# Half-tile weight buffers three tiles ahead, and seven products instead of eight in one more column group

## The chip, the cores and the metric

The kernel runs on one core of a Trainium2 chip. The time is device microseconds of one launch; the kernel before took 945.35 us (median of 3 runs, 945.0 to 945.57). A profile is one execution recorded by the hardware, on which every engine's instructions have a start and a duration.

## The reference, cut to what matters

The program is a two-layer encoder on 256 tokens of width 1024, all in float32. A layer has a gated feed-forward block, attention, and a second feed-forward block:

```python
x = x + 0.5 * swiglu(rms_norm(x, ffn1_norm[l]), ffn1_w_gate[l], ffn1_w_up[l], ffn1_w_down[l])
h = rms_norm(x, mix_norm[l]);  proj = h @ w_in[l]          # then two kinds of attention, and @ w_out[l]
x = x + 0.5 * swiglu(rms_norm(x, ffn2_norm[l]), ffn2_w_gate[l], ffn2_w_up[l], ffn2_w_down[l])

def swiglu(h, w_gate, w_up, w_down):
    return (jax.nn.silu(h @ w_gate) * (h @ w_up)) @ w_down
```

The hidden width is 2816. So there are four feed-forward blocks, and their weights (three matrices of 1024 x 2816 each) are by far most of what is read and multiplied.

## The kernel before, in words

**Precision.** Every operand of a matrix product is split in two, a rounded high part and the remainder (low). A product is three matmuls: high x high, low x high, high x low. ScalarE makes the high part of a weight (a cast, `act.copy`), VectorE the low part (a subtraction), in `emit_split` (line 167). The two are in buffers named `whi` and `wlo`, three of each, each of a whole tile.

**Weight tiles.** A tile is 512 rows of a weight matrix by 512 columns, 1 MB, laid out as 128 partitions x 4 x 512. One list, `specs`, holds the tiles in the order in which TensorE uses them. `emit_dma` loads a tile into one of six `raw` buffers; `ahead` (line 198) issues loads, preparations and splits; `weights` (line 219) is called when a tile's use begins and has the splits issued up to `LOOK = 2` tiles further. Each split is issued as two instructions of 128 x 1024 on ScalarE and two on VectorE.

**A feed-forward block** (`ffn`, line 547) goes over the hidden columns in five groups of 512 (numbers 0 to 4) and a last one of 256. In group n the gate and up products are made (4 tiles x 4 row blocks x 2 token blocks x 3 = 96 matmuls of 512 columns), and the hidden activations of group n-1 are transposed (`turn`) and multiplied by two tiles of the down matrix (`down`, 48 matmuls).

**Groups by seven products.** In groups 2 and 4 (`SEVEN`) gate and up are computed together as a 2 x 2 block product (token halves by input halves, input halves by gate and up) with seven block products in place of eight: 84 matmuls in place of 96 (`by_seven`, line 579). For this, seven weight tiles are split instead of four: four as loaded or with a second matrix added while it is loaded (`gather`, a load issued by GpSimd that adds into the buffer), three more made from buffers already there by additions on VectorE (`plus`, two instructions of 128 x 1024). The token operands that the sums need are made once for each block, in four steps during group 1 (`make_sums`, line 304). The order of the tiles in such a group, with the letters of `seven` (line 115): a, b, b again after an addition, the first down tile, d, d again after an addition, a again after a load has been added, c, the second down tile. The down product's first use needs the transposed activations of the group before, whose low part VectorE writes in `turn`.

**Order.** Outside the attention each engine runs its instructions in the order in which the program issues them (`keep_in_program_order`, line 50, which is why most instructions of the profile carry the line L50). So when `weights()` is called before a product, the splits that it triggers stand ahead, in ScalarE's and VectorE's queues, of everything that is issued after that product. In the attention a scheduler may reorder.

**Constants** for the attention are made in the first block, from `aside` at the start of group 3: eleven small instructions on VectorE, one exponential on ScalarE, and a transpose on TensorE (`attention_constants`, line 454).

Here are the functions that the change touches:

Of the kernel before, what the change touches and what calls it, by code (L numbers as in the profile page):

```python
# [14 lines left out]
P = 128  # L15
# [9 lines left out]
QA, KA, VA, QB, KB, VB = 0, 512, 640, 768, 1280, 1792  # L25
BIG = 1e33

LOOK, AHEAD = 2, 8
N_RAW, N_HI, N_LO = 6, 3, 3
N_S4 = 16  # L30
SEVEN = (2, 4)


@with_exitstack
def trunk(ctx: ExitStack, tc: tile.TileContext, x, n1, g1, u1, d1, nm, w_in, sink,
# [31 lines left out]
    def nm_(s):  # L67
        uid[0] += 1
        return f"{s}_{uid[0]}"
# [94 lines left out]
        if s.behind is not None:  # L164
            s.behind()

    def emit_split(i):
        s = specs[i]
        kn, n, raw = s.kn, s.n, raws[s.src]
# [3 lines left out]
        cuts = [0, kn // 2, kn] if i > 1 and (i not in fine or kn < 4) else [kn * j // 4 for j in range(5)]  # L173
        for a, b in zip(cuts, cuts[1:]):
            if n == D:
                views = [(t[0][:, a:b, c:c + 512], t[1][:, a:b, c:c + 512], t[2][:, a:b, c:c + 512])
                         for t in [(raw, hi, lo)] for c in (0, 512)]
            elif i not in paired:
                views = [(raw[:, a:b], hi[:, a:b], lo[:, a:b])]
            else:  # L180
                views = [(raw.rearrange("p k (s c d) -> p c k s d", s=2, c=2)[:, c, a:b],
                          hi.rearrange("p k (c s d) -> p c k s d", s=2, c=2)[:, c, a:b],
                          lo.rearrange("p k (c s d) -> p c k s d", s=2, c=2)[:, c, a:b]) for c in range(2)]
            for r_, h_, l_ in views:
                act.copy(h_, r_)
                dve.tensor_tensor(l_, r_, f(h_), op=ALU.subtract)
            if i < 2:
                yield
        for k in s.free:
            raws.pop(k)  # L190

    def emit_early(i):
        yield from emit_dma(i)
        yield from emit_split(i)

    at = dict(use=0, dma=2, prep=2, split=2)

    def ahead(n):

        n = min(n, len(specs) - 1)  # L200
        while True:
            if at["split"] <= n and at["prep"] > at["split"]:
                for _ in emit_split(at["split"]):
                    pass
                at["split"] += 1
            elif at["prep"] <= min(n + 1, len(specs) - 1) and at["dma"] > at["prep"] and \
                    (specs[at["prep"]].prep is None or at["split"] >= at["prep"]):
# [65 lines left out]
    class Norm:  # L273
# [115 lines left out]
    def take_x(k):  # L389
# [8 lines left out]
        elif k == 1:  # L398
            for e in (g, u, g, u):
                next(e)  # L400
            norm.pair(2)
            ahead(2)
            norm.pair(3)
        elif k == 2:
            ahead(3)
# [65 lines left out]
            dve.tensor_scalar_mul(gsub[:, l:l + 1], gcol[:, 48 + l:49 + l], 1.0 - lam_init[l])  # L471


    def tokens(accs, xs, w, k0, ks=range(4), first=0, last=KC - 1, order=None):

        hi, lo = w
        for k, t in (order or [(k, t) for k in ks for t in range(2)]):
            kk = k0 + k
            xv = xs[kk // 2][:, kk % 2]
            xh, xl = xv[:, t * P:(t + 1) * P], xv[:, S + t * P:S + (t + 1) * P]  # L480
            pe.matmul(accs[t], lhsT=xh, rhs=hi[:, k], start=kk == first, stop=False)
            pe.matmul(accs[t], lhsT=xl, rhs=hi[:, k], start=False, stop=False)
            pe.matmul(accs[t], lhsT=xh, rhs=lo[:, k], start=False, stop=kk == (last if isinstance(last, int) else last[t]))

    def split(dst, src, scale=None):

# [7 lines left out]

    def narrow(acc, w, j, xs, kcs, first, last):

        hi, lo = w
        for i, (wk, xk) in enumerate(kcs):
            wh = hi[:, wk, j * P:(j + 1) * P]
            wl = lo[:, wk, j * P:(j + 1) * P]  # L500
# [46 lines left out]
    def ffn(norm, aside=None, before=None, final=False):  # L547
# [19 lines left out]
            return h  # L567

        def prod(xo, w):
            hi, lo = w  # L570
            acc = bank()
            for k in range(4):
                xh, xl = xo(k)
                pe.matmul(acc, lhsT=xh, rhs=hi[:, k], start=k == 0, stop=False)
                pe.matmul(acc, lhsT=xl, rhs=hi[:, k], start=False, stop=False)
                pe.matmul(acc, lhsT=xh, rhs=lo[:, k], start=False, stop=k == 3)
            return acc

        def by_seven(h, g):
# [57 lines left out]
        if before is None:  # L637
            before = norm.late
        before(0)
        ws = (weights(), weights(LOOK - 1))  # L640
        for k in (0, 2):
            if k:
                before(1)
# [40 lines left out]
    def ffn_end(parts, last):  # L684
# [4 lines left out]
        w = {0: weights()}  # L689

        def group(h, order, a=None, c=slice(None), first=0):
            tokens(a or accs[h], hT, [t[:, :, c] for t in w[h]], G4, first=first, last=last[h], order=order)

        def tail(h, order=BY_TOKENS, a=None, c=slice(None)):
            tokens(a or accs[h], [None] * (2 * NGRP) + hE, [t[:, h, :, c] for t in w["rest"]], 4 * NGRP, last=last[h], order=order)
# [4 lines left out]
        w["rest"] = [t.rearrange("p k (h n) -> p h k n", h=2) for t in weights()]  # L700
        w[1] = weights(LOOK - 1)
        return group, tail

    def ffn_close(parts, nxt):
# [4 lines left out]
        for t in range(2):  # L709
            res.add(0, t)  # L710
        tail(1)
        ahead(at["use"] + LOOK - 1)
        group(1, [(1, t) for t in range(2)])
        for j in range(2):
            nxt.pair(j)
# [7 lines left out]
    def mix(l, norm, nxt_norm):  # L723
# [68 lines left out]
            return e  # L792


        s0, s1 = first_groups(norm, (weights(), weights(LOOK - 1)))
# [39 lines left out]
        vB = tp.tile([P, 2, 512], F32, tag="v", bufs=1, name=nm_("v"))  # L835
        vsl = [bank() for _ in range(2)]
        for k0 in (0, 4):
            hi, lo = weights()
            for k in range(4):
                kk = k0 + k  # L840
                xv = norm.xs[kk // 2][:, kk % 2]
                for t in range(2):
                    xh, xl = xv[:, t * P:(t + 1) * P], xv[:, S + t * P:S + (t + 1) * P]
                    pe.matmul(vsl[t], lhsT=xh, rhs=hi[:, k], start=kk == 0, stop=False)
                    pe.matmul(vsl[t], lhsT=xl, rhs=hi[:, k], start=False, stop=False)
                    pe.matmul(vsl[t], lhsT=xh, rhs=lo[:, k], start=False, stop=kk == KC - 1)
# [73 lines left out]
        res = Residual(nxt_norm, accs)  # L920

        def out_part(w, k0, h, order=None):
            tokens(accs[h], oT, [t.rearrange("p k (h n) -> p h k n", h=2)[:, h] for t in w], k0, range(2), 4, 3, order)

        w = weights()
        for h in range(2):
# [112 lines left out]
```

## Time and profile before

| | |
|---|---|
| Median of 3 runs | 945.35 us |
| Profiled execution | 945.94 us, of which the span of the trace is 944.2 us |
| TensorE (matmul) busy | 931.5 us, 99% |
| VectorE busy | 718.6 us, 76% |
| ScalarE busy | 538.1 us, 57% |
| DMA read | 184.32 MB at 196 GB/s over the span |
| Granted TensorE clock | 0.999 |

Busy shares are means over the whole span; a stage can look different. In the trace's timelines the first number is the start in us from the span's start, the second the duration of the row, then engine, line, operation, the names of what is written and read, and how many instructions the row merges. Matmuls overlap: one of 512 columns shows some 0.39 us, and the next starts 0.227 us after it. The four feed-forward blocks begin near 5, 290, 485 and 755 us.

### The profile page before, as it was taken

The numbers are of one execution on the slowest core, as the hardware profiler recorded it, in microseconds if no ns is written. First come the engines' busy times: TensorE is split into PE (matmuls) and PEld (weight loads), VectorE is DVE, ScalarE is ACT, GpSimd is POOL, SyncE is SP. The second block draws the span as 40 slices with busy tenths as digits, with TensorE's granted clock in tenths as the row PEclk, the third lists the DMA queues.
The fourth block names the chain that finished last, engine by engine and source line by source line (L and its number), as shares of the span: only waits on it lengthen the run. The fifth ranks groups of instructions, "written<-read, shape, count | busy, mean of one in ns | idle before, by whom it ended". The sixth has DMA issues, their size and how long they took to land.

```text
span 944.2 us, 12633 instructions
## 1 busy us (share of the span) xinstructions
PE 931.5 (99%) x4844; PEld 790.4 (84%) x4844; DVE 718.6 (76%) x1086; ACT 538.1 (57%) x853; POOL 40.6 (4%) x65
## 2 busy tenths in 40 slices
PE   8999999999999999999999999999999999999997
PEld 6887888899888887888888888888999888888886
DVE  5689779579856589679557995887796667995983
ACT  6647546567735547446554564656676464564653
POOL 0400000000000000000000000000000000000001
PEclk9999999999999999999999999999999999999999
DMA  9959868655424829958557498586551447497631
GB/s 336 338 140 286 246 178 303 190 179 136 134 90 144 256 92 286 293 133 306 185 179 223 97 329 243 148 300 186 170 168 56 139 174 223 104 346 241 151 118 45
DMA packets 106669, 186.19 MB, mean 197 GB/s; under 512 B 3438, under 2 KB 31152, under 8 KB 106608
## 3 DMA queue, kind: packets, MB, share of 16 engines
q1 hardware_dynamic: 96816, 167.27, 52.0%
q0 software_dynamic: 8704, 17.07, 10.5%
q10 hardware_dynamic: 1088, 1.05, 0.3%
q8 instruction: 38, 0.62, 0.3%
q14 instruction: 23, 0.19, 0.1%
HBM read 184.32 MB, written 1.05 MB: 196 GB/s over the span
## 4 chain that ended last, share of the span: by engine, by line
PE 82%; DVE 11%; ACT 4%; issue 2%; DMA 0%; ACTq 0%; POOLq 0%; POOL 0%; DVEq 0%
PE ps L50 82%; DVE wlo L50 6%; DVE tmp L50 3%; ACT whi L50 3%; DVE s L50 1%; ACT s L50 1%; DVE raw L50 0%; DMA xk<-in_x_dram 0%; ACT tmp L50 0%; DVE xk L50 0%; ACTq L50 0%; POOLq L1034 0%; POOL rf L50 0%; DVE rf L50 0%; DVEq L50 0%
## 5 line engine op out<-in xcount | busy, mean ns | idle before, releaser
L50 PE MATMUL ps<-whi,s 128*128 128x512 f32 (+1 forms) x2252 | 699.4, 391 | 2.0 <-DVE s L50 2.0
L50 DVE TENSOR_TENSOR wlo<-raw,whi 128x1024 fp32r<-128x1024 f32 (+2 forms) x440 | 433.8, 1034 | 97.7 <-ACT whi L50 95.1
L50 PEld LDWEIGHTS ps<-whi,s 128*128 128x128 f32 x2252 | 419.7, 188 | 88.4 <-DVE s L50 3.7
L50 ACT CAST whi<-raw 128x1024 fp32r<-128x1024 f32 (+2 forms) x440 | 372.0, 902 | 177.2 <-PE ps L50 117.7
L50 PE MATMUL ps<-wlo,s 128*128 128x512 f32 (+1 forms) x1126 | 438.1, 389 | 0.0
L50 PEld LDWEIGHTS ps<-wlo,s 128*128 128x128 f32 x1126 | 211.8, 188 | 43.9 <-DVE wlo L50 0.2
L50 PE MATMUL ps<-s,whi 128*128 128x256 f32 x448 | 82.7, 286 | 0.0
L50 PEld LDWEIGHTS ps<-s,whi 128*128 128x128 f32 x448 | 70.1, 192 | 1.1
L50 ACT CAST s<-ps 128x512 fp32r<-128x512 f32 x48 | 26.0, 589 | 66.0 <-PE ps L50 66.0
L50 PE MATMUL ps<-s,wlo 128*128 128x256 f32 x224 | 63.3, 283 | 0.0
L50 DVE TENSOR_TENSOR s<-ps,s 128x512 fp32r<-128x512 f32 x48 | 31.0, 685 | 41.5 <-ACT s L50 41.5
L50 PEld LDWEIGHTS ps<-s,wlo 128*128 128x128 f32 x224 | 42.9, 192 | 0.0
L50 ACT CAST s<-tmp 128x512 fp32r<-128x512 f32 (+1 forms) x22 | 13.2, 602 | 49.1 <-DVE tmp L50 49.1
L50 PE MATMUL ps<-ident,s 128*128 128x128 f32 x304 | 39.6, 273 | 0.0
L50 PEld LDWEIGHTS ps<-ident,s 128*128 128x128 f32 x304 | 35.1, 141 | 4.7
L50 POOL DMA_DIRECT2D raw<-in_ffn_w_up_dram x16 | 20.8, 1298 | 412.9 <-ACT whi L50 120.0
L50 DVE TENSOR_TENSOR raw<-raw,raw 128x1024 f32<-128x1024 f32 x32 | 37.6, 1218 | 0.0
L50 ACT ACTIVATE s<-s,negm 128x256 f32<-128x256 f32 x64 | 31.8, 501 | 7.4 <-DVE negm L50 7.4
L50 ACT ACTIVATE tmp<-ps,r 128x512 f32<-128x512 f32 (+1 forms) x32 | 19.9, 636 | 28.0 <-PE ps L50 27.9
L50 DVE SCALAR_TENSOR_TENSOR s<-ps,hr,tmp 128x512 f32<-128x512 f32 (+1 forms) x32 | 20.8, 681 | 13.4 <-PE ps L50 6.9
L50 ACT ACTIVATE s<-ps,gcol 128x256 fp32r<-128x256 f32 x48 | 19.3, 474 | 19.7 <-PE ps L50 19.7
L50 DVE SCALAR_TENSOR_TENSOR s<-ps,gcol,s 128x256 fp32r<-128x256 f32 x48 | 20.3, 477 | 13.1 <-ACT s L50 13.0
(104 smaller groups left out, 411.2 us busy)
## 6 DMA issues: line engine op xcount, KB each, us to landing
raw<-in_ffn_w_down_dram SPq DMA_DIRECT2D x44, 1024.0 KB, 5.2
raw<-in_ffn_w_gate_dram SPq DMA_DIRECT2D x39, 1024.0 KB, 6.2
raw<-in_ffn_w_up_dram SPq DMA_DIRECT2D x39, 1024.0 KB, 5.1
raw<-in_ffn_w_up_dram POOLq DMA_DIRECT2D x16, 1024.0 KB, 9.1
raw<-in_w_in_dram SPq DMA_DIRECT2D x14, 1024.0 KB, 5.1
raw<-in_ffn_w_gate_dram SPq DMA_DIRECT2D x8, 512.0 KB, 3.8
raw<-in_ffn_w_up_dram SPq DMA_DIRECT2D x8, 512.0 KB, 5.0
raw<-in_w_in_dram SPq DMA_DIRECT2D x8, 512.0 KB, 4.5
```

Of the source, the lines that this page charges most:

```text
L50: ins = issue(*a, **k)
```

## The change

Four things change together.

1. The split weights live in 14 buffers of half a tile (seven pairs of high and low) instead of six of a whole tile. `emit_split(i, j)` splits one half; `ahead` counts in halves. When a tile's use begins the halves up to six further are issued (`HALVES`), and when its second half is first used (`part`) one more. This is up to three tiles ahead, where it was two.
2. `SEVEN` becomes (2, 3, 4): group 3 of each block goes by seven products too.
3. The four sums of x are kept in buffers that the attention uses for other things (tags `q` and `v`), and the common pool `s4` has 14 buffers instead of 16.
4. `AHEAD`, how many tiles further the load list is looked at, becomes 10 instead of 8; the `raw` buffers stay six.

Some splits change form: the four tiles with the last 256 rows of the down matrices are split in 2 instructions of 1024 elements instead of 4 of 512 (8 in all, for 16 before), and the four paired tiles of the attention's projection in 4 of 512 instead of 8 of 256.

```diff
-LOOK, AHEAD = 2, 8
-N_RAW, N_HI, N_LO = 6, 3, 3
-N_S4 = 16
-SEVEN = (2, 4)
+AHEAD = 10
+N_RAW, N_W = 6, 14
+N_S4 = 14
+SEVEN = (2, 3, 4)
...
-    def emit_split(i):
+    class Split:
+        def __init__(self, i):
+            self.i, self.n, self.parts, self.held = i, specs[i].n, [], False
+
+        def part(self, k, c=slice(None), h=None):
+            if h is None:
+                h, k = divmod(k, 2)
+            if h and not self.held:
+                self.held = True
+                ahead(2 * self.i + 1 + HALVES)
+            return [t[:, k, c] for t in self.parts[h]]
+
+    def emit_split(i, j):
...
-        hi = wp.tile([P, kn, n], F32R, tag="whi", bufs=N_HI, name=nm_("whi"))
-        lo = wp.tile([P, kn, n], F32R, tag="wlo", bufs=N_LO, name=nm_("wlo"))
-        loaded[i] = (hi, lo)
...
+        shape = (P, 8, P) if s.n == 256 else (P, 2, 512)
+        hi, lo = [wp.tile(list(shape), F32R, tag="w", bufs=N_W, name=nm_("w")) for _ in range(2)]
+        loaded[i].parts.append((hi, lo))
...
+    HALVES = N_W // 2 - 1
...
-    def weights(look=LOOK):
+    def weights(less=0, held=False):
+
         i = at["use"]
         at["use"] += 1
         if i > 1:
-            ahead(i + look)
-        return loaded.pop(i)
+            ahead(2 * i + HALVES - less)
+        w = loaded[i]
+        w.held = held
+        return w
...
-                sm = blk().rearrange("p a (c s) -> p (a c) s", c=2)
+                tag, n = ("q", 3) if len(self.sm) < 3 else ("v", 1)
+                sm = tp.tile([P, 2, 512], F32R, tag=tag, bufs=n, name=nm_(tag)).rearrange("p a (c s) -> p (a c) s", c=2)
...
         def prod(xo, w):
-            hi, lo = w
             acc = bank()
             for k in range(4):
+                hi, lo = w.part(k)
                 xh, xl = xo(k)
```

The other lines of the diff hand the halves to the products in the same way (`tokens`, `narrow`, the value projection of the attention).

More of the change, by code (lines that the diff above doesn't have):

```diff
@@ new lines, in emit_split @@
+    def emit_split(i, j):
+        s = specs[i]
+        raw = raws[s.src]
+        if j == 0:
+            loaded[i] = Split(i)
+        shape = (P, 8, P) if s.n == 256 else (P, 2, 512)
+        hi, lo = [wp.tile(list(shape), F32R, tag="w", bufs=N_W, name=nm_("w")) for _ in range(2)]
+        loaded[i].parts.append((hi, lo))
+        if s.n == D:
+            raw = raw[:, :, j * 512:(j + 1) * 512]
+        elif i in paired:
+            raw = raw.rearrange("p k (s c d) -> p c k s d", s=2, c=2)[:, j]
+            hi, lo = [t.rearrange("p k (s d) -> p k s d", s=2) for t in (hi, lo)]
+        elif s.n == 256:
+            raw = raw[:, :, j * P:(j + 1) * P]
+        else:
+            raw = raw[:, 2 * j:2 * j + 2]
+        m = shape[1] // 2 if i < 2 or i in fine else shape[1]
+        for a in range(0, shape[1], m):
+            r_, h_, l_ = [t[:, a:a + m] for t in (raw, hi, lo)]
+            act.copy(h_, r_)
+            dve.tensor_tensor(l_, r_, f(h_), op=ALU.subtract)
@@ L187, in emit_split @@
             if i < 2:
                 yield
-        for k in s.free:
-            raws.pop(k)
+        if j == 1:
+            for k in s.free:
+                raws.pop(k)
     def emit_early(i):
         yield from emit_dma(i)
-        yield from emit_split(i)
-    at = dict(use=0, dma=2, prep=2, split=2)
+        for j in range(2):
+            yield from emit_split(i, j)
+    HALVES = N_W // 2 - 1
+    at = dict(use=0, dma=2, prep=2, split=4)
     def ahead(n):
-        n = min(n, len(specs) - 1)
+        n = min(n, 2 * len(specs) - 1)
@@ L201, in ahead @@
         while True:
-            if at["split"] <= n and at["prep"] > at["split"]:
-                for _ in emit_split(at["split"]):
+            if at["split"] <= n and at["prep"] > at["split"] // 2:
+                for _ in emit_split(*divmod(at["split"], 2)):
                     pass
                 at["split"] += 1
-            elif at["prep"] <= min(n + 1, len(specs) - 1) and at["dma"] > at["prep"] and \
-                    (specs[at["prep"]].prep is None or at["split"] >= at["prep"]):
+            elif at["prep"] <= min(n // 2 + 1, len(specs) - 1) and at["dma"] > at["prep"] and \
+                    (specs[at["prep"]].prep is None or at["split"] >= 2 * at["prep"]):
@@ L401, in take_x @@
             norm.pair(2)
-            ahead(2)
+            ahead(5)
             norm.pair(3)
         elif k == 2:
-            ahead(3)
+            ahead(7)
             for t in range(2):
@@ L471, in attention_constants, with tokens @@
             dve.tensor_scalar_mul(gsub[:, l:l + 1], gcol[:, 48 + l:49 + l], 1.0 - lam_init[l])
-    def tokens(accs, xs, w, k0, ks=range(4), first=0, last=KC - 1, order=None):
-        hi, lo = w
+    def tokens(accs, xs, w, k0, ks=range(4), first=0, last=KC - 1, order=None, cols=slice(None), h=None):
         for k, t in (order or [(k, t) for k in ks for t in range(2)]):
             kk = k0 + k
+            hi, lo = w.part(k, cols, h)
             xv = xs[kk // 2][:, kk % 2]
             xh, xl = xv[:, t * P:(t + 1) * P], xv[:, S + t * P:S + (t + 1) * P]
-            pe.matmul(accs[t], lhsT=xh, rhs=hi[:, k], start=kk == first, stop=False)
-            pe.matmul(accs[t], lhsT=xl, rhs=hi[:, k], start=False, stop=False)
-            pe.matmul(accs[t], lhsT=xh, rhs=lo[:, k], start=False, stop=kk == (last if isinstance(last, int) else last[t]))
+            pe.matmul(accs[t], lhsT=xh, rhs=hi, start=kk == first, stop=False)
+            pe.matmul(accs[t], lhsT=xl, rhs=hi, start=False, stop=False)
+            pe.matmul(accs[t], lhsT=xh, rhs=lo, start=False, stop=kk == (last if isinstance(last, int) else last[t]))
     def split(dst, src, scale=None):
@@ L495, in narrow @@
     def narrow(acc, w, j, xs, kcs, first, last):
-        hi, lo = w
         for i, (wk, xk) in enumerate(kcs):
-            wh = hi[:, wk, j * P:(j + 1) * P]
-            wl = lo[:, wk, j * P:(j + 1) * P]
+            wh, wl = w.part(wk, h=j)
             xv = xs[xk // 2][:, xk % 2]
@@ L569, in prod @@
         def prod(xo, w):
-            hi, lo = w
             acc = bank()
             for k in range(4):
+                hi, lo = w.part(k)
                 xh, xl = xo(k)
-                pe.matmul(acc, lhsT=xh, rhs=hi[:, k], start=k == 0, stop=False)
-                pe.matmul(acc, lhsT=xl, rhs=hi[:, k], start=False, stop=False)
-                pe.matmul(acc, lhsT=xh, rhs=lo[:, k], start=False, stop=k == 3)
+                pe.matmul(acc, lhsT=xh, rhs=hi, start=k == 0, stop=False)
+                pe.matmul(acc, lhsT=xl, rhs=hi, start=False, stop=False)
+                pe.matmul(acc, lhsT=xh, rhs=lo, start=False, stop=k == 3)
             return acc
@@ L639, in ffn @@
         before(0)
-        ws = (weights(), weights(LOOK - 1))
+        ws = (weights(), weights(2))
         for k in (0, 2):
@@ L691, in group @@
         def group(h, order, a=None, c=slice(None), first=0):
-            tokens(a or accs[h], hT, [t[:, :, c] for t in w[h]], G4, first=first, last=last[h], order=order)
+            tokens(a or accs[h], hT, w[h], G4, first=first, last=last[h], order=order, cols=c)
         def tail(h, order=BY_TOKENS, a=None, c=slice(None)):
-            tokens(a or accs[h], [None] * (2 * NGRP) + hE, [t[:, h, :, c] for t in w["rest"]], 4 * NGRP, last=last[h], order=order)
+            tokens(a or accs[h], [None] * (2 * NGRP) + hE, w["rest"], 4 * NGRP, last=last[h], order=order, cols=c, h=h)
         group(0, [(k, t) for k in range(3) for t in range(2)])
@@ L699, in ffn_end @@
         group(0, [(3, t) for t in range(2)])
-        w["rest"] = [t.rearrange("p k (h n) -> p h k n", h=2) for t in weights()]
-        w[1] = weights(LOOK - 1)
+        w["rest"] = weights()
+        w[1] = weights(2)
         return group, tail
@@ L711, in ffn_close @@
         tail(1)
-        ahead(at["use"] + LOOK - 1)
+        ahead(2 * at["use"] - 2 + HALVES)
         group(1, [(1, t) for t in range(2)])
@@ L792, in soft_a @@
             return e
-        s0, s1 = first_groups(norm, (weights(), weights(LOOK - 1)))
+        s0, s1 = first_groups(norm, (weights(held=True), weights(2, True)))
         kept[0] = False
@@ L837, in mix @@
         for k0 in (0, 4):
-            hi, lo = weights()
+            w = weights()
             for k in range(4):
                 kk = k0 + k
+                hi, lo = w.part(k)
                 xv = norm.xs[kk // 2][:, kk % 2]
@@ L843, in mix @@
                     xh, xl = xv[:, t * P:(t + 1) * P], xv[:, S + t * P:S + (t + 1) * P]
-                    pe.matmul(vsl[t], lhsT=xh, rhs=hi[:, k], start=kk == 0, stop=False)
-                    pe.matmul(vsl[t], lhsT=xl, rhs=hi[:, k], start=False, stop=False)
-                    pe.matmul(vsl[t], lhsT=xh, rhs=lo[:, k], start=False, stop=kk == KC - 1)
+                    pe.matmul(vsl[t], lhsT=xh, rhs=hi, start=kk == 0, stop=False)
+                    pe.matmul(vsl[t], lhsT=xl, rhs=hi, start=False, stop=False)
+                    pe.matmul(vsl[t], lhsT=xh, rhs=lo, start=False, stop=kk == KC - 1)
             if k0 == 0:
@@ L922, in out_part @@
         def out_part(w, k0, h, order=None):
-            tokens(accs[h], oT, [t.rearrange("p k (h n) -> p h k n", h=2)[:, h] for t in w], k0, range(2), 4, 3, order)
+            tokens(accs[h], oT, w, k0, range(2), 4, 3, order, h=h)
         w = weights()
```

15 lines of the change are left out of this document (removed).

## The prediction

> **What bounds the kernel now.** I read the page's busy times first, then TensorE's waits, then the stages of the second feed-forward block, then the chain and VectorE's timeline in them.
>
> ```profile
> PE 931.5 (99%) x4844; PEld 790.4 (84%) x4844; DVE 718.6 (76%) x1086; ACT 538.1 (57%) x853; POOL 40.6 (4%) x65
> L50 DVE TENSOR_TENSOR wlo<-raw,whi 128x1024 fp32r<-128x1024 f32 (+2 forms) x440 | 433.8, 1034 | 97.7 <-ACT whi L50 95.1
> L50 DVE TENSOR_TENSOR raw<-raw,raw 128x1024 f32<-128x1024 f32 x32 | 37.6, 1218 | 0.0
> raw<-in_ffn_w_up_dram SPq DMA_DIRECT2D x39, 1024.0 KB, 5.1
> raw<-in_ffn_w_up_dram POOLq DMA_DIRECT2D x16, 1024.0 KB, 9.1
> ```
>
> ```profile
> PE ps L50 <- DVE s L50: 2.0, 4, 0.5
> ```
>
> TensorE is busy 99% and, after the first 6 us, waits only four times, 0.5 us each: once per feed-forward block, for VectorE's `s`. So the kernel is bound by TensorE, with VectorE just behind it at one place. Below are groups 1, 2 (seven products), 3 (eight) and 4 (seven) of the second block.
>
> ```profile
> 314.50:348.00 33.50, 33.50 (x154) 27.83 (x152) 26.31 (x41) 15.68 (x20) 1.32 (x1) 1.00 0.64 189
> 348.00:379.60 31.60, 31.09 (x141) 25.53 (x140) 31.37 (x33) 21.18 (x24) 1.28 (x1) 1.00 0.76 235
> 379.60:413.20 33.60, 33.60 (x154) 27.89 (x153) 21.56 (x21) 14.26 (x17) 1.28 (x1) 1.00 0.71 218
> 413.20:444.00 30.80, 30.80 (x142) 25.58 (x141) 28.80 (x31) 20.90 (x24) 1.28 (x1) 1.00 0.83 256
> ```
>
> The columns are the stretch, then busy time of TensorE, its weight loads, VectorE, ScalarE, GpSimd. With seven products TensorE needs 30.8 us, with eight 33.5; but VectorE is then busy 31.37 of 31.60 us. Group 3 is where it catches up (21.56 of 33.60). The place of the wait is at the end of this chain:
>
> ```profile
> 321.03 0.59 ACT s L50
> 322.60 2.36 DVE wlo L50 x2
> ...
> 329.11 2.36 DVE wlo L50 x2
> ...
> 350.12 1.15 DVE raw L50
> ...
> 354.95 1.95 DVE wlo L50 x2
> 356.89 0.33 issue
> 357.23 0.70 DVE s L50
> ```
>
> From the transposes of group 0's activations (321.03) to the low part of group 1's (`turn`, 357.23 to 357.93) VectorE or the cast that feeds it is always the one waited for. The first down product of group 2 waits for that last row.
>
> **Part by part.** The changed kernel's instructions, listed in the order in which each engine gets them, give the counts: 48 matmuls fewer, VectorE 44 more, ScalarE 4 more, GpSimd 8 accumulating loads more.
>
> *Matmuls removed.* 12 per block at 0.227 us (one starts 0.227 after the other) are 2.7 us, which is 33.5 - 30.8; four blocks, 10.9 us. All of it is on the path, since TensorE never idles in group 3.
>
> *VectorE's work in a group of seven*, from its own timeline, start to start:
>
> ```profile
> 358.43 2.35 DVE L50 TENSOR_TENSOR wlo<-raw,whi 128x1024 fp32r<-128x1024 f32 x2
> 360.69 2.36 DVE L50 TENSOR_TENSOR raw<-raw,raw 128x1024 f32<-128x1024 f32 x2
> 362.96 1.41 DVE L50 TENSOR_TENSOR tmp<-ps,tmp 128x512 f32<-128x512 f32 x2
> ```
>
> A tile's split, or a pair of additions, takes 2.27 us (358.43 to 360.69). Nine splits (20.4), two pairs of additions (4.5), seven sums of products (4.3: a pair of 1.3, a pair of 1.2, three of 0.6), two `up` (1.3) and `turn` (1.2) are 31.8 us, against TensorE's 30.8. Before, the deficit was repaid in group 3. Now three such groups stand in a row.
>
> *The new wait: `turn` behind the next splits.* The deeper lookahead has an effect that the counts don't show. `turn` is issued after the second product, whose `weights` and `part` now issue splits three tiles ahead. So in VectorE's order `turn` stands behind the split of d and behind the two additions that make the second d; before, it stood ahead of both. VectorE runs in issue order, so the first down product waits for them too. What it has to do between two `turn`s is:
> - Group 2. The stretch 321 to 357.93 keeps seven splits (d's in place of one that now fits in ahead of the first `turn`, where VectorE idles 3.1 us before 321.16), the sums of x and one pair of additions; it gains the second pair, 2.27 us. The last half of group 1's first down tile must wait for a buffer (seven halves back: the first half of the tile begun at 320.70, released near 323.6, then a cast of 1.06), which costs another 0.95. So `turn` ends near 361.1, and TensorE waits 3.7 us instead of 0.5: 3.2 more.
> - Groups 3 and 4. One whole cycle of 31.8 us lies between two `turn`s. After its wait TensorE frees buffers late: c's second half waits for d's first (0.25 us idle), the second down tile's second half for a cast behind the first silu (0.6), the next a's second half for a cast behind the second silu, which waits for VectorE (0.65), and 0.2 at smaller ones. 33.5 us against 30.8: TensorE waits 2.7 us in each. Bounds: with no idle 31.8, so 1.0; above, below.
>
> Queued behind the waiting matmul are all later products; the splits behind `turn` wait for nothing of it.
>
> *Sum of a block:* -2.7 + 3.2 + 2.7 + 2.7 = 5.9 us longer; four blocks 23.6.
>
> *Constants in the first block.* On VectorE these run from 98.96 to the next split at 102.93, 4.0 us, in a group that had room; now they stand inside group 3's cycle, between two splits that `turn` follows. The silu table's reload (1.28 on ScalarE) adds some 0.8 behind the silu. 4.8 us; 4.0 with nothing from the reload.
>
> *Added loads.* b of a following group starts when the additions into d have ended, just before `turn`, and is followed by the accumulating load: 5.1 + 0.6 (SP to GpSimd, 319.35 to 319.96) + 9.1 = 14.8 us after; VectorE comes to b's split some 17 us after `turn`, its cast 15. Hidden, by about 1 us. Were the load 3 us later, most of that would fall on both cycles of each block.
>
> *Attention.* Four `s4` blocks fewer are asked for in the blocks and two fewer exist. TensorE's order there differs by some transposes moved; no wait of TensorE stands there before. 0, between -1 and +3 us per layer (nearest row: the 0.5 us waits). The larger splits of the tail tiles and of the paired tiles save VectorE 24 instructions, hidden by TensorE, 0. `AHEAD` alone moves nothing, as six `raw` buffers limit the loads.
>
> *Total:* 23.6 + 4.8 = 28 us. The profiled execution took 945.94, 0.6 over the median; from the median of 945.35, **973 us**.
>
> *A rule weighed against a row.* The Trainium skill's page "VectorE: DVE Perf Modes" (section on the TRN2 errata) gives a float32 `tensor_tensor` as (N + 151)/0.96 ns, 1224 ns for 1024; the trace's mean agrees (1218), but neighbours start 1.13 us apart. Charged by that page, 22 such instructions per cycle would add 2.0 us to each of eight cycles, an estimate of 989 us instead of 973. I go by the starts.
>
> **Rivals.**
> - *TensorE stays the bound* (faster). If VectorE had 3.2 us more room before group 2's `turn`, and each cycle came below 30.8, only the removed matmuls would count: 945.4 - 10.9 = 934.5 us. For it: the lookahead lets VectorE work ahead, and it idles in group 0 (a gap of 5.1 us before 312.11). Against: the chain starts at TensorE's transposes at 321, behind which no earlier idle time can be used. It decides once `turn` is ready 9.1 us after the group begins. At 1 to 2 us of wait in all per block the change would be lost in 0.2% (about 2 us, what a measurement of this kernel can tell from no change).
> - *Small loss:* none of the waits for buffers; -2.7 + 2.3 + 1.0 + 1.0 = 1.5 per block, with the constants 10 us: 956.
> - *The clock.* At the start matmuls are slow:
>
> ```profile
> 7.23 0.63 PE L50 MATMUL ps<-wlo,s 128*128 128x512 f32 x1
> 11.69 0.39 PE L50 MATMUL ps<-wlo,s 128*128 128x512 f32 x1
> ```
>
> Ten or so, from 6.2 to 10.5 us, start up to 0.43 apart instead of 0.23, 2 us lost, though the granted clock reads 1.00. If each of my twelve waits brought this back, 24 us more: 997. Against: the waits of 0.5 us are followed by normal spacing. The Trainium skill ("TensorE: Matmul & The Clock Gate", "What's actually happening") has the array go to half speed after an idle window of about 3.4 us; my waits lie around that, and no run here shows a wait of that length.
> - *The accumulating load comes 3 us late* in eight cycles: up to 24 us, 997.
>
> **How the numbers follow.** Late `turn`, between 956 and 990: 0.74. The clock: 0.10. The late load: 0.05. TensorE the bound: 0.08. No change: 0.03. The range 953 to 998 leaves out the two last and the tails. Slower 0.89, same 0.03, faster 0.08.
>
> **What would show it.** In the changed kernel's waits: TensorE for VectorE's `s`, twelve times, 2.6 to 3.7 us, one of them (first block, group 3) near 7. A chain that runs through VectorE from group 1's start to group 4's first down product; `turn` right after a pair of `raw` additions; groups 2 to 4 of some 34.5, 33.5 and 33.5 us. Wrong would be: four waits as before and groups of 30.8 (TensorE the bound), `wlo` waiting for DMA (the load), or matmuls of 0.63 after the waits (the clock).

## The result: 4.4% slower, and the profile after

The changed kernel takes 987.38 us (median of 4 runs, 986.4 to 987.96); the kernel before, run beside it, 945.46 us (945.0 to 945.74). The ratio is 1.0443, 95% interval 1.0425 to 1.0461: 41.9 us more. 973 us was predicted, with a range of 953 to 998. The direction and the place were right, and some 14 us were missing. The profiled execution after has a span of 984.6 us, 40.4 more than before.

First the page's busy times, the groups that answer to those shown of before, and the load that adds to its target:

```profile
PE 936.3 (95%) x4796; PEld 789.7 (80%) x4796; DVE 783.3 (80%) x1130; ACT 567.0 (58%) x857; POOL 51.9 (5%) x73
L50 DVE TENSOR_TENSOR w<-raw,w 128x1024 fp32r<-128x1024 f32 (+1 forms) x440 | 468.9, 1094 | 102.2 <-ACT w L50 98.2
L50 DVE TENSOR_TENSOR raw<-raw,raw 128x1024 f32<-128x1024 f32 x48 | 56.5, 1217 | 0.0
raw<-in_ffn_w_up_dram POOLq DMA_DIRECT2D x24, 1024.0 KB, 9.6
```

TensorE has 48 matmuls fewer than before and is yet busy 4.8 us longer: some of its matmuls must have become slower. VectorE has 64.7 us more to do. TensorE's waits:

```profile
PE ps L50 <- DVE s L50: 34.0, 13, 4.1
PE ps L50 <- DMA grow<-in_ffn_norm_dram: 3.5, 1, 3.5
PE ps L50 <- ACT tmp L50: 3.4, 2, 2.9
```

Waits for `s` went from 2.0 to 34.0 us, and 3.4 us for `tmp` are new in the first block: there the product behind the transposes waits until ScalarE has copied the group's first product out of its accumulation bank. The wait at the start (`grow`) is as before. Groups 1 and 2 (in part), then the cycles into groups 3 and 4 of the second block and into group 4 of the fourth, each from the start of one wait to the start of the next; the columns are as in the stages before, with the granted clock after GpSimd:

```profile
334.00:372.20 38.20, 38.20 (x177) 31.52 (x175) 31.66 (x45) 19.78 (x25) 1.29 (x1) 1.00 0.58 143
372.20:408.20 36.00, 32.76 (x141) 26.67 (x140) 33.04 (x35) 20.79 (x23) 2.57 (x2) 0.95 0.83 233
408.20:443.20 35.00, 32.55 (x141) 26.58 (x140) 32.15 (x34) 20.79 (x23) 2.57 (x2) 0.95 0.86 241
889.80:923.40 33.60, 31.15 (x141) 25.52 (x140) 32.13 (x34) 20.91 (x23) 2.57 (x2) 1.00 0.90 249
```

The second and third rows are one cycle each, from one late `turn` to the next: 36.0 and 35.0 us for 141 matmuls and transposes, where a group of seven took 30.8 before. TensorE is idle 3.24 and 2.45 us of them, and the clock stood at 0.95 on average. The last row is a cycle at full clock: 33.60 us, with the same 2.45 us of waiting. So the slower matmuls make the cycle longer, and the wait at its end does not shrink for it (it is 2.45 us after the third row and 2.46 after the last). Where that 0.95 comes from shows in shorter stretches behind the waits:

```profile
372.80:376.20 3.40, 0.69 (x3) 0.60 (x4) 3.40 (x5) 2.28 (x3) 0.00 (x0) 1.00 0.75 252
376.20:379.60 3.40, 3.40 (x10) 2.62 (x9) 3.37 (x5) 0.77 (x1) 0.00 (x0) 0.50 0.90 305
379.60:383.00 3.40, 3.40 (x16) 2.79 (x16) 2.40 (x3) 1.57 (x2) 1.28 (x1) 1.00 0.96 313
410.40:413.80 3.40, 3.11 (x8) 2.48 (x9) 3.40 (x5) 1.74 (x2) 0.00 (x0) 0.51 0.84 267
445.70:449.10 3.40, 3.40 (x15) 2.78 (x16) 3.38 (x4) 2.16 (x3) 0.00 (x0) 1.00 0.90 274
```

After the wait that ends at 375.51 the clock is at one half for 3.4 us (10 matmuls in place of 16), and after that full again. The wait of 2.45 us that ends at 410.69 is followed by the same; the wait of 2.45 us that ends at 445.67 is not.

VectorE's timeline at the late `turn` of group 2:

```profile
365.69 6.90 DVE L50 TENSOR_TENSOR w<-raw,w 128x1024 fp32r<-128x1024 f32 x6 [0.26 <-PE ps L50]
372.50 2.35 DVE L50 TENSOR_TENSOR raw<-raw,raw 128x1024 f32<-128x1024 f32 x2
374.78 1.28 DVE L50 TENSOR_TENSOR s<-ps,s 128x512 fp32r<-128x512 f32 x2
```

The order is the predicted one: three splits, the two additions for d, and only then `turn`, on whose first half (375.47) the matmul at 375.51 had waited since 372.27. And the chain into group 4:

```profile
407.77 2.28 DVE raw L50 x2
410.06 5.11 DMA raw<-in_ffn_w_up_dram
...
415.73 9.96 DMA raw<-in_ffn_w_up_dram
...
425.99 1.04 ACT w L50
...
442.75 2.27 DVE raw L50 x2
445.01 0.61 DVE s L50
445.67 4.42 PE ps L50 x18
```

Between 410.06 and 425.69 it runs through b's load and the load that adds c to it, which the prediction had called hidden by about 1 us. They start when the additions have ended (they free b's old buffer), and the next additions can't be made before b is split: a second loop, here as long as VectorE's own.

Put together from the profiled executions: 48 matmuls at 0.227 us, 10.9 us less; waits for `s` and `tmp` 37.4 in place of 2.0 us, 35.4 more; together 24.5 of the 40.4 us. The other 15.9 go by the clock: 0.982 over 984.6 us is 17.7 us not granted, before 0.9 (0.999 over 944.2); a small part of it fell on idle time. The busy time of TensorE says much the same: 936.3 us, where 931.5 less 10.9 were to be expected, is 15.7 more.

### The profile page after: what moved, and what is told of

It reads as the page before. It is cut to its first block, busy times and chain, and to the rows that moved or that the text cites. A ratio compares the mean times of both kernels' runs of the same rounds, so it can differ in the third digit from the quotient of the medians.

```text
span 984.6 us, 12989 instructions
## 1 busy us (share of the span) xinstructions
PE 936.3 (95%) x4796; PEld 789.7 (80%) x4796; DVE 783.3 (80%) x1130; ACT 567.0 (58%) x857; POOL 51.9 (5%) x73
## 3 DMA queue, kind: packets, MB, share of 16 engines
q10 hardware_dynamic: 1088, 1.05, 0.3%
HBM read 192.71 MB, written 1.05 MB: 197 GB/s over the span
## 4 chain that ended last, share of the span: by engine, by line
PE 69%; DVE 16%; DMA 9%; issue 4%; ACT 1%; SPq 0%; POOLq 0%; DVEq 0%; POOL 0%; ACTq 0%
PE ps L50 69%; DMA raw<-in_ffn_w_up_dram 8%; DVE w L50 8%; DVE raw L50 5%; DVE s L50 2%; DVE tmp L50 1%; ACT w L50 1%; DMA raw<-in_ffn_w_gate_dram 1%; DVE distA L50 0%; ACT tmp L50 0%; SPq L162 0%; DVE distB L50 0%; DVE xk L50 0%; DVEq L50 0%; POOLq L1057 0%
## 5 line engine op out<-in xcount | busy, mean ns | idle before, releaser
L50 PE MATMUL ps<-w,s 128*128 128x512 f32 (+1 forms) x2754 | 651.6, 395 | 33.3 <-DVE s L50 33.2
L50 PEld LDWEIGHTS ps<-w,s 128*128 128x128 f32 x2754 | 520.2, 191 | 146.5 <-DVE s L50 38.5
L50 DVE TENSOR_TENSOR w<-raw,w 128x1024 fp32r<-128x1024 f32 (+1 forms) x440 | 468.9, 1094 | 102.2 <-ACT w L50 98.2
L50 ACT CAST w<-raw 128x1024 fp32r<-128x1024 f32 (+1 forms) x440 | 400.2, 946 | 231.0 <-PE ps L50 149.4
L50 PE MATMUL ps<-w,q 128*128 128x512 f32 x432 | 106.8, 397 | 3.5 <-ACT tmp L50 3.4
L50 PEld LDWEIGHTS ps<-w,q 128*128 128x128 f32 x432 | 81.2, 190 | 20.7 <-ACT tmp L50 4.2
L50 PE MATMUL ps<-s,w 128*128 128x256 f32 x672 | 84.0, 285 | 0.0
L50 PEld LDWEIGHTS ps<-s,w 128*128 128x128 f32 x672 | 81.7, 192 | 1.1
L50 PE MATMUL ps<-w,v 128*128 128x512 f32 x144 | 34.6, 389 | 0.0
L50 DVE TENSOR_TENSOR tmp<-ps,tmp 128x512 f32<-128x512 f32 x48 | 32.9, 685 | 0.4
L50 ACT CAST q<-tmp 128x512 fp32r<-128x512 f32 x20 | 12.4, 620 | 35.0 <-DVE tmp L50 35.0
```

The source lines that it names most:

```text
L50: ins = issue(*a, **k)
```

## The experiments

My theory after the result: the late `turn` makes the waits, the waits make the slow matmuls, and nothing else costs. Its rivals: groups of seven in a row are too much for VectorE or for the loads wherever `turn` stands. All ratios below are to the kernel before on the same chip, whose time was 945 to 946 us.

### `turn` ahead again, and the third group alone

In the first kernel the second product no longer triggers splits further ahead; `turn` is issued before d's split and additions.

```diff
-            p7 = prod(norm.summed(2), weights())
+            p7 = prod(norm.summed(2), weights(1, True))
```

> The changed kernel with one call altered: the second product of a group of seven asks for one half-tile less and holds back the request at its second half, so that turn is issued ahead of d's split and of the additions into d, as in the kernel before. Theory (the late turn costs the waits): turn of group 2 ends 4.5 us earlier than TensorE needs it less 3.2 - 0.5, so TensorE waits at most 0.5 us in group 2, and in groups 3 and 4 only for VectorE's surplus of 31.8 over 30.8 us, about 1 us each at most. No wait is long enough for slow matmuls. Per block -2.7 + 1 to 1.5; with some 4 us for the constants in the first block: 936 to 946 us, against 987. Rival (three groups of seven are too much for VectorE whatever the order): the waits move to other products, 2 us or more in each of groups 3 and 4, and the time stays over 965.

991.1 us, ratio 1.0481 [1.0464, 1.0499]: the theory fell. The rival's time (over 965) and place (groups 3 and 4) held, but not its reason, VectorE: the chain shows the loads. TensorE still waits, now at the transposes of `turn` in groups 3 and 4, for the hidden activations of the group before. The chain, in the second block:

```profile
375.44 5.26 DMA raw<-in_ffn_w_up_dram
...
381.26 13.08 DMA raw<-in_ffn_w_up_dram
...
394.44 1.06 ACT w L50
...
410.08 2.28 DVE raw L50 x2
412.38 5.12 DMA raw<-in_ffn_w_up_dram
```

Each load of b starts when the additions into d have ended. From one such start to the next (375.44 to 412.38) are 36.9 us, 18.9 of them in the two loads of b. ScalarE stands idle for 4.88 us until b is there and its cast can begin at 394.44. With `turn` early nothing else holds the group, and this loop is the bound.

The second kernel is the kernel before with group 3 by seven products, and nothing else changed:

```diff
-SEVEN = (2, 4)
+SEVEN = (2, 3, 4)
```

> The kernel before (whole-tile buffers, two tiles ahead) with group 3 by seven products as well, nothing else. Theory: turn stands ahead of d's split here, so groups 2 to 4 wait 0.5, 1 and 1 us for VectorE's surplus; -2.7 + 2 per block and 4 us for the constants: 942 to 952. Rival (the third group is itself the cause): 965 or more, with waits of 2 us and over in groups 3 and 4.

983.45 us (980.5 to 988.45), 1.0408 [1.0375, 1.0442], the rival's result. The chain in the second block is the same loop:

```profile
373.23 2.28 DVE raw L50 x2
375.53 5.12 DMA raw<-in_ffn_w_up_dram
...
381.21 13.52 DMA raw<-in_ffn_w_up_dram
...
409.20 2.28 DVE raw L50 x2
411.50 5.02 DMA raw<-in_ffn_w_up_dram
```

So the third group of seven costs some 38 us in the old order and buffers too. The new lookahead isn't what makes it slow; it only decides which of two loops holds it.

### The buffers without the third group

After, with two groups of seven as before, first with the late and then with the early `turn`:

```diff
-SEVEN = (2, 3, 4)
+SEVEN = (2, 4)
```

> The changed kernel's buffers and lookahead with only groups 2 and 4 by seven products. Theory: group 2's wait of 3.2 us stays as it is (its cause lies in group 1 and in the order), and slow matmuls follow most of these waits, 1.7 us each; group 4 waits 0 to 1 us since VectorE catches up in group 3. Per block 2.7 + 1 to 1.7 + 0 to 1: 958 to 966. Rival (the buffers do no harm, the third group does): 945 plus or minus 2.

965.69 us, 1.0215 [1.02, 1.023], as the theory had it.

```profile
PE ps L50 <- DVE s L50: 14.3, 8, 3.3
```

These are 3.25 us in each group 2 and 0.33 in each group 4: behind a group of eight VectorE has caught up. 12.3 us more waits than before; the clock of 0.991 over a span of 963.6 us is 8.7 us not granted, 7.8 more than before. Together 20.1, against 19.4 between the two spans.

```diff
-SEVEN = (2, 3, 4)
+SEVEN = (2, 4)
...
-            p7 = prod(norm.summed(2), weights())
+            p7 = prod(norm.summed(2), weights(1, True))
```

> The changed buffers with groups 2 and 4 by seven products, and turn issued ahead of d's split and additions. With the late turn this took 965.7 us, with a wait of 3.2 us per block for VectorE's s. Theory (the order alone made that wait): group 2 waits 0 to 0.5 us, no slow matmuls follow, 943 to 947. Rival (the half-tile buffers hold VectorE or ScalarE up whatever the order): waits of 2 us or more remain and the time is over 955.

942.36 us (6 runs, 941.7 to 942.49), 0.9966 [0.9955, 0.9978], a little under the 943 to 947 of the theory. This is faster than both kernels, by 3.1 us or so against before. No wait for `s` is left:

```profile
PE ps L50 <- DMA grow<-in_ffn_norm_dram: 3.1, 1, 3.1
PE ps L50 <- ACT tmp L50: 0.5, 1, 0.5
```

One call changed, 23.3 us apart: with two groups of seven, the late `turn` is the whole loss, and without it the buffers win back the four waits of 0.5 us that the kernel before had (2.0 of the 3.1 us).

### The price of the clock

The changed kernel with the third product (`p6`) of each group of seven computed twice into the same bank, which adds 144 matmuls (32.7 us) just where TensorE waits for `turn`:

```diff
-        def prod(xo, w):
+        def prod(xo, w, times=1):
...
-            for k in range(4):
+            for k in list(range(4)) * times:
...
-            p6 = prod(norm.summed(1), weights())
+            p6 = prod(norm.summed(1), weights(), 2)
```

> The changed kernel with the product ahead of the wait (p6) computed twice into the same bank, the second time from zero again, so the result is the same and TensorE has 12 matmuls (2.7 us) more in each of the twelve groups, just where it waits. Theory (the waits are VectorE's, and TensorE's slow matmuls after them cost about 15 us): the added matmuls fill the waits, TensorE does not slow down, the granted clock is 0.995 or more instead of 0.982, and the kernel is faster for the added work: 971 to 977 us. Rival (the slow matmuls have another cause, or cost nothing): clock as before and 986 to 990, or, if the added work does not fit in the waits, up to 1010.

977.47 us (974.68 to 985.31), 1.0353 [1.0306, 1.0399]: 10 us faster than the changed kernel, with 32.7 us more to compute. The four runs scatter more than others do, and why one took 985.31 us, at a clock of 0.995, is open; the trace is of a run of 975.59.

```profile
PE 954.3 (98%) x4940; PEld 806.9 (83%) x4940; DVE 783.2 (80%) x1130; ACT 567.4 (58%) x857; POOL 51.7 (5%) x73
PE ps L50 <- DVE s L50: 5.9, 8, 1.4
PE ps L50 <- ACT tmp L50: 2.9, 1, 2.9
```

TensorE's waits fell from 37.4 to 8.8 us, its clock rose from 0.982 to 0.998. Work added less waits saved would make the span 4.1 us longer (32.7 - 28.6); it is 10.8 us shorter (973.8 for 984.6). The difference, 14.9 us, is what the half clock had cost, next to the 15.9 of the sum above. VectorE's busy time is unchanged (783.2 us); TensorE is merely kept busy over its wait.

### Which loop holds the three groups

Seven `raw` buffers in place of six let b be loaded one tile earlier (two `s4` buffers fewer make the room). Once with the late `turn`, once with the early:

```diff
-N_RAW, N_W = 6, 14
-N_S4 = 14
+N_RAW, N_W = 7, 14
+N_S4 = 12
```

> The changed kernel with seven raw buffers instead of six (and 12 s4 buffers, to make room), turn late as in the change. Theory (two loops of much the same length: VectorE's with the late turn, and the one from the additions that free b's buffer over its load, the accumulating load and back to those additions; both have to go): cutting the load's loop alone leaves VectorE's of 33.5 us and the waits of group 2, 3.2: 978 to 988 us. Rival (the load's loop is all that limits groups 3 and 4): 955 to 968.

983.14 us, 1.0404 [1.0389, 1.042], as the theory of the two loops had it. In the second to fourth block the waits are 3.24, 2.44 and 2.44 us as in the changed kernel, but the loads are all but off the chain, whose shares by engine are:

```profile
PE 78%; DVE 15%; issue 4%; DMA 2%; ACT 1%; POOLq 0%; ACTq 0%; DVEq 0%; POOL 0%
```

So with the late `turn` VectorE's loop alone gives these waits. The loop of the loads is level with it in the changed kernel, no longer. The 4.2 us between the two kernels go with 1.4 us fewer waits, all in the first block, and with the clock (0.986 for 0.982).

```diff
-N_RAW, N_W = 6, 14
-N_S4 = 14
+N_RAW, N_W = 7, 14
+N_S4 = 12
...
-            p7 = prod(norm.summed(2), weights())
+            p7 = prod(norm.summed(2), weights(1, True))
```

> Both: seven raw buffers and turn ahead of d's split and additions. Theory of the two loops: b's load now starts when the first down tile has been split, some 4.5 us earlier, and is hidden; turn is in time; only VectorE's 31.8 against 30.8 us and the constants are left: 936 to 947 us. Rival (the loads themselves are too many, six plain and two accumulating ones in 30.8 us): b's split still waits for DMA, cycles of 33 us or more, 955 or over.

955.47 us, 1.0112 [1.0094, 1.0131], the rival's time (955 or over). With both loops opened 32 us of the 42 are gone, but not the last 10; the chain still goes through b's loads:

```profile
393.58 5.96 DMA raw<-in_ffn_w_up_dram
...
400.10 12.23 DMA raw<-in_ffn_w_up_dram
```

This kernel with the constants moved behind group 4 of the first block:

```diff
-            if n == 3 and aside is not None:
-                aside()
...
+        if aside is not None:
+            aside()
```

> As the one before, with the attention's constants made after group 4 instead of at the start of group 3, where VectorE has room again. Theory: 2 to 5 us less than the kernel without this, since they stand in VectorE's chain of the first block: 932 to 943 us. Rival (the first block has room for them): no difference, within 1 us.

951.38 us, 1.0066 [1.0051, 1.0081]: 4.1 us less, the difference that the theory gave; its 932 to 943 us were missed, since they went by the time expected of the kernel before this one. In the traces the waits of the first block's groups 3 and 4 fall from 5.7 to 3.0 us. Another 1.5 us fall in the fourth block (3.47 to 1.95 at its last transposes), where no constants are made, so not all of the 4.1 need be theirs. Its waits for `s` are still 12.4 us, about 1.05 and 1.95 at the transposes of groups 3 and 4 in each block. Is it the load that adds c to b? That load left out (the factor of this product is then another matrix):

```diff
-                Step(4, 512, load(b), key=b, behind=gather(c, b), free=[]),
+                Step(4, 512, load(b), key=b, free=[]),
```

> The kernel with seven raw buffers, the early `turn` and the constants behind group 4 (951.4 us), without the one accumulating load that stands behind b's load (c into b; twelve of the 24 accumulating loads; the other, b into a, stays). The second factor of that product is then another matrix, so the output is not the reference's; matmuls, splits and additions are as many. Theory: what still makes TensorE wait 12.4 us there, at the transposes of groups 3 and 4, is b's split coming late behind that accumulating load (10 to 12 us each). Then the waits shrink to 2 us or less in all and the time is 936 to 943 us. Rival: VectorE's own work per group (31.8 us by my count against 30.8 of TensorE's) is the limit, so that without the load it still loses about 1 us in each of eight groups: 947 to 951 us.

950.42 us, 1.0057 [1.004, 1.0074]. The theory fell and the rival held: the waits stay (12.2 us). The chain by line has next to no DMA left, and the cycle from group 3 to group 4 in the second block is this:

```profile
by line: PE ps L50 80.4%; issue 5.3%; ACT w L50 4.8%; DVE w L50 3.2%; DVE tmp L50 2.0%; DVE raw L50 1.6%; DVE s L50 1.0%; DMA xk<-in_x_dram 0.4%; ACT tmp L50 0.3%; ACTq L50 0.2%; DVEq L50 0.1%; DVE xk L50 0.1%; POOLq L1057 0.1%; POOL rf L50
387.00:420.50 33.50, 31.48 (x143) 25.70 (x142) 32.23 (x34) 20.54 (x24) 1.28 (x1) 1.00 0.74 221
```

VectorE is busy 32.23 of 33.50 us. The other 1.27 hold two idle pieces of 0.60 behind casts that stand behind a silu on ScalarE:

```profile
406.49 1.22 DVE L50 TENSOR_TENSOR w<-raw,w 128x1024 fp32r<-128x1024 f32 x1 [0.60 <-ACT w L50]
410.05 1.23 DVE L50 TENSOR_TENSOR w<-raw,w 128x1024 fp32r<-128x1024 f32 x1 [0.60 <-ACT w L50]
```

By this trace it is the limit under both loops: with the rest out of the way a cycle of seven takes VectorE, with the casts that it waits for, 33.4 us, and TensorE 30.8. No run with less work for VectorE confirmed it.

Two attempts to get below it failed. Eight `raw` buffers, paid for with four half-tile buffers (base: the kernel of 951.38 us):

```diff
-N_RAW, N_W = 7, 14
+N_RAW, N_W = 8, 10
```

> The same kernel of 951.4 us with eight raw buffers, for which the split weights have ten half-tile buffers in place of fourteen (the lookahead falls from six halves to four, which is two tiles, as in the kernel before). Theory that the loads start too late for want of raw buffers: b is loaded a further tile earlier, so b's split no longer waits, and the time falls to 938 to 946 us. Rival: the accumulating load's own length and the shorter lookahead decide; then the splits are held by their buffers and the time is 951 to 965 us.

957.88 us, 1.0131 [1.0114, 1.0148], inside the rival's numbers. TensorE's wait is now for `tmp`, at the product right behind the transposes; ScalarE's copy of the group's first product, which it waits for, stands behind casts that wait for VectorE's additions:

```profile
PE ps L50 <- ACT tmp L50: 16.3, 12, 2.0
```

The loads are off its chain, too. Whether the shorter lookahead alone makes these waits was not separated.

And the second pair of additions on GpSimd (same base):

```diff
-        def plus(x, to):
+        def plus(x, to, eng=dve):
...
-                    dve.tensor_tensor(t_, t_, x_, op=ALU.add)
+                    eng.tensor_tensor(t_, t_, x_, op=ALU.add)
...
-                Step(**n, prep=plus(b, d), src=d, free=[b, d]),
+                Step(**n, prep=plus(b, d, pool), src=d, free=[b, d]),
```

> The kernel of 951.4 us (seven raw buffers, early `turn`, constants behind group 4), with the second pair of additions of each group of seven (b into d) made on GpSimd instead of VectorE. A product of 128 x 512 takes GpSimd 1.29 us in the trace of before, so the pair would take it some 5 us. Theory: VectorE's own work in such a group (32.2 of 33.5 us busy in the kernel without the sum's load) sets the cycle of groups 3 and 4. Without this pair it falls by 2.3 us to about 31.2, next to TensorE's 30.8: the waits of 1.0 and 2.0 us at the transposes go to 0.5 or less, and the time is 936 to 942 us. Rival: the additions end later (5 us instead of 2.3), b's load and the splits of d with them, or VectorE's instructions become longer beside GpSimd's; then the waits move there and the time is 950 to 975 us.

976.25 us, 1.0319 [1.0302, 1.0337], what the rival described, a little above its 950 to 975. First the timeline of GpSimd, then of ScalarE and of VectorE:

```profile
402.33 5.60 POOL L50 TENSOR_TENSOR raw<-raw,raw 128x1024 f32<-128x1024 f32 x2 [6.45 <-DVE w L50]
```

```profile
405.61 1.05 ACT L50 CAST w<-raw 128x1024 fp32r<-128x1024 f32 x1 [5.15 <-POOL raw L50]
```

```profile
406.69 3.59 DVE L50 TENSOR_TENSOR w<-raw,w 128x1024 fp32r<-128x1024 f32 x2 [3.37 <-ACT w L50]
```

The pair takes 5.6 us there. The cast of the sum waits for it on ScalarE, and VectorE, whose next instruction is that tile's split, stands still for 3.37 us: more than the 2.3 us that it was spared.

## Why the prediction was right, and what it missed

- **Matmuls removed.** 48 fewer, 10.9 us of work, as predicted; moving `SEVEN` back (965.69 for 987.38 us) shows that this gain is lost many times over.
- **The late `turn`.** Right in place, order and cause: 13 waits for VectorE's `s` where twelve were forecast, `turn` directly behind a pair of `raw` additions. 3.24 us in group 2 (forecast 3.7) and 2.45 in groups 3 and 4 (forecast 2.7). A block was to become 5.9 us longer; by these waits it is 4.9 (3.24 + 2.45 + 2.45 - 0.5 - 2.7). The runs with two groups of seven, late and early, show the cause for group 2 by itself.
- **VectorE's cycle.** 31.8 us of work and 33.5 with the waits for buffers were forecast; the one cycle from group 3 to group 4 at full clock took 33.60, with VectorE busy for 32.13, and the kernel without c's load shows 33.4 as VectorE's own limit, with 32.23 us of work and idle pieces of 0.60 at the two silus. Moving `turn` ahead doesn't make this go away: for groups in a row it only moves the wait to the transposes.
- **Constants.** 4.8 forecast. The changed kernel's first block waits 13.0 us in all (13.9 by the forecast), each later block 8.1: 4.9 more. The size was right, the way only in part: the one wait "near 7" came as several, and 2.88 us of them are the wait for `tmp` in group 3. ScalarE's exponential for the constants, which waits for VectorE until 106.27, stands ahead of the copy that frees the bank (108.26).
- **The accumulating load "hidden by about 1 us".** This cover was thin. In the changed kernel the chain runs through it, with no loss of its own in the second to fourth block, since seven buffers leave the waits at 2.44. But as soon as `turn` is early it is the bound (36.9 us a cycle, 991.1 us). The load takes 8.6 to 10.7 us in the median in these kernels, but 10 to 15 in these groups, where other loads are under way.
- **Attention 0.** Between the same matmuls of both traces each attention is 0.4 to 0.5 us shorter.
- **The clock: the step that failed.** The sum charged nothing for it ("the waits of 0.5 us are followed by normal spacing") and put 0.10 on a rival of +24 us. It measured 15 to 16 us: 15.9 left over in the sum, 15.7 in TensorE's busy time, 14.9 in the kernel whose wait was filled. The waits of 0.5 us said nothing of waits of 2.5 to 3.2: six of the nine waits of the later three blocks were followed by half clock. The 1.00 that the prediction read at the start says little: in the trace of before the record of the clock begins only at 10.60 us, just as 17 matmuls begin in 3.4 us where 9 began in the 3.3 before. The rest of the sum was 28.4 us and came to 24.5; with the 14.9 of the filled kernel that is 39.4, next to the 40.4 between the two spans. The medians lie 1.5 us further apart than these two executions.

By the rule of the Trainium skill that the rival went by ("TensorE: Matmul & The Clock Gate", section "What's actually happening") the array goes to half speed after at least one idle window of about 3.4 us, and the window runs free of the kernel. The trace agrees with the length (3.4 us at 0.50 behind the wait, then full speed) and with the free run (of two waits of 2.45 us in the second block one was followed by it, the other not). It differs in the threshold: no wait of that block was as long as 3.4 us, and waits of 2.45 and 3.24 were enough. The measurement decides.

The estimate of 989 us that the prediction gave by the page "VectorE: DVE Perf Modes" (section on the TRN2 errata) lies nearer to the result than 973, but not for its reason: it would have made the waits longer, and they came out shorter than forecast.

## What to carry to other kernels

A deeper lookahead changes the order in an engine that runs in issue order: ask for each call that prefetches what small, urgent instruction is issued after it, and put the call behind that. When an engine just below its limit repays a deficit in a stage that is now to be changed too, compute the cycle in which nothing is repaid, for that engine and for every loop of buffer, load and use, since removing one loop only shows the next (here: late `turn`, then b's load, then VectorE's own 33.4 us). And charge a wait of 2 to 3 us on TensorE with up to half of another 3.4 us of slow matmuls behind it; twelve waits of 1.4 us in the mean, as in the kernel with eight `raw` buffers, left the clock at 0.997.

## What the runs showed of the hardware that I had not expected

- Waits of TensorE well below 3.4 us bring the half clock: 2.45 us sufficed in some blocks of the changed kernel and not in others, and in the first block a wait of 3.24 us (74.21 to 77.45) passed without it. What decides is where the wait lies in a grid of 3.41 us. Within a run the granted clock changes only on such a grid, and the grid lies differently from run to run. The kernel with the late `turn` and two groups of seven has the same first wait (3.27 us from 74.18). The changed kernel first, then that one, each cut at its own grid:

```profile
72.39:75.81 3.42, 1.82 (x9) 1.16 (x7) 3.42 (x4) 1.45 (x4) 0.00 (x0) 1.00 0.75 222
75.81:79.22 3.41, 1.77 (x8) 1.46 (x9) 3.41 (x5) 2.99 (x3) 0.00 (x0) 1.00 0.65 183
79.22:82.63 3.41, 3.41 (x17) 2.83 (x16) 3.38 (x4) 1.05 (x1) 0.30 (x1) 1.00 0.87 299
72.12:75.53 3.41, 2.06 (x10) 1.36 (x8) 3.41 (x4) 1.65 (x3) 0.00 (x0) 1.00 1.06 259
75.53:78.95 3.42, 1.51 (x6) 1.24 (x7) 3.42 (x5) 3.04 (x3) 0.00 (x0) 1.00 0.63 181
78.95:82.36 3.41, 3.41 (x10) 2.63 (x8) 3.38 (x5) 1.04 (x1) 0.00 (x0) 0.50 0.96 304
```

Idle for 1.60 and 1.64 us of two stretches, TensorE kept the full clock; idle for 1.35 and 1.91, it was at one half in the third. Over all the traces here, from the first record of the clock on, each such stretch at full clock with 2.0 us or more of idle time was followed by half clock, none with less than 1.5 was, and between these both happened.
- More work can take less time: 32.7 us of extra matmuls in place of waiting made the kernel 10 us faster.
- A load of 1 MB that adds to its target, 8.6 to 10.7 us in the median, took 13.08, 13.52 and 15.34 us in the chains of the kernels with the early `turn` and with the third group alone. Around the first of these (374 to 396 us) plain loads moved 4.93 MB; that they are the cause was not separated.
- GpSimd adds two 128 x 1024 float32 operands in 2.82 us (mean of 24), VectorE in 1.22.
